# Layer 1's score matmuls: both maps' chunks in pairs, and the low queries' products on half of the array's rows each

## The chip, the cores and the metric

The kernel runs on one core of one Trainium2 chip. The metric is the device time of one execution in microseconds (us); lower is better. The kernel is written in Python against a tile framework: the program lists instructions and tiles, and the framework adds the waits, assigns buffers and orders the instructions of each engine by a plan of its own, so that the order on an engine can differ a little from the order in the program.

## The reference

Two layers over x of 2048 tokens by 1024. Layer 0 has a sliding-window attention and a chunked attention with a position bias; layer 1 has a differential attention. The change touches the scores of layer 1 alone. There, each of 8 heads has two maps of queries and keys, 64 wide:

```python
def block(i):                      # 128 queries
    qchunk = (start + jnp.arange(Q_BLOCK)) // CHUNK          # CHUNK = 64
    mask = (kchunk[None, :] <= qchunk[:, None])[None, None]
    s1 = jnp.einsum('bqhd,bkhd->bhqk', qb1, k1).astype(jnp.float32) * scale
    s2 = jnp.einsum('bqhd,bkhd->bhqk', qb2, k2).astype(jnp.float32) * scale
    p1 = jax.nn.softmax(jnp.where(mask, s1, NEG_INF), axis=-1)
    p2 = jax.nn.softmax(jnp.where(mask, s2, NEG_INF), axis=-1)
    a = p1 - lam * p2
    return jnp.einsum('bhqk,bkhd->bqhd', a.astype(v.dtype), v)
```

The result is normalised per head, multiplied by a SiLU gate, projected and added to the residual stream.

## The kernel before, in words

All of it is float32 at the borders. Products that need more than one rounded operand are split: a number is kept as a high part H and a low part L, both in a rounded 32-bit form (`F32R`), and a product is the sum of HH, HL and LH (`mm3`, lines 214 to 216: three matmuls into one PSUM bank).

Layer 0 (`project(0)`, `mix0`) and the projection of layer 1 (`project(1)`) come first. Then `_mix1` runs layer 1's attention, gates and output projection together. Names in it:

- A head `h` and a query block `b` of 512 tokens are one unit of `heads()`; the order is blocks 0 and 1 of every head, then block 2 of every head, then block 3. A block has four query tiles `j` of 128 tokens (`NTB` = 4). Query tile t = 4b + j sees (t + 1) * 128 keys, cut into chunks `z` of up to 512 keys (`cuts`); the last one can be 128, 256, 384 or 512 wide.
- `scores` makes, for each `j`, the scores of both maps `m`. The queries come in `qd` (high parts) and `ql` (low parts), each with the same 64 rows in both halves of the 128 rows. The key tile `K[z, m]` has the high part of map m's keys in rows m*64 to m*64+63 and the low part in the other 64 rows. So one matmul of `qd` with the key tile gives qH*kH + qH*kL (line 919), and one of `ql` with it gives qL*kH + qL*kL (line 920), in the same PSUM bank of the pool `pS`, which has four banks.
- After the two matmuls of a chunk, VectorE (DVE) masks 64 queries of the last chunk (line 922) and takes the row maximum `nm` (line 923); ScalarE (ACT) makes the exponential with that bias and its sum, out of PSUM into a tile `cP` (line 926), and that frees the bank. Map 0's chunks all come first, then map 1's.
- At the end of a query tile, a few small instructions make the factors `rl` and `e` (lines 934 to 940). `combine` is put off until the first exponential of the next query tile: ACT scales map 1's chunks (line 956), GpSimd (POOL) scales map 0's and adds (lines 957, 958).
- `then(j, m, z)` issues loads on SyncE's DMA queue at fixed places: the next queries at the third query tile, the next head's key tiles `ck` (lines 1044, 1045) and the values `cv` (line 1051) at the last one.
- `values` transposes the probabilities (line 970), copies them out of PSUM on DVE (line 972) and multiplies with the values (line 974). `gate` and `split` finish a head. `gates()` makes the gate's projection and `projected` the output projection, both by `mm3`; these are the side work.
- `pace` weaves the three: it takes a piece of scores (a piece says how much work it was, `yield wd / 256`), lets the values trail by `LAG1`, and hands out side work in a share of the work done (`STAGES1`). The side work's matmuls are placed behind `self.anchor`, the last score matmul issued so far (`issue_after`).

Of the kernel before, what the change touches and what calls it, by code (L numbers as in the profile page):

```python
# [10 lines left out]
F32 = mybir.dt.float32  # L11
F32R = mybir.dt.float32r
AF = mybir.ActivationFunctionType
# [5 lines left out]
P = 128  # L19
S = 2048  # L20
# [5 lines left out]
HD = 64  # L26
# [60 lines left out]
class Trunk:  # L87
# [776 lines left out]
    def _mix1(self, es):  # L864
        nc, tc, a, s = self.nc, self.tc, self.a, self.s1
        n = "c"
# [6 lines left out]
        pp = pool("pp", 20)  # L873
        kp = pool("kp", 4)
        sb = pool("sb", 2)
        NS, NTR, NO, NM = self.BANKS1
        pS = pool("pS", NS, space=PSUM)
# [3 lines left out]
        mm = nc.tensor.matmul  # L881

        def small(tag, m=1):
            return sm.tile([P, m], F32, tag=tag, name=n + tag)
# [12 lines left out]
        def scores(h, b, q, K, res, then):  # L897


            qd, ql = q  # L900
            us = res["u"] = []
            for j in range(NTB):
                t = b * NTB + j
                nk = (t + 1) * P
                cuts = [(c, min(nk, c + 512)) for c in range(0, nk, 512)]
                nb = len(cuts)
                js = slice(j * P, (j + 1) * P)
                nm = small("nm", 8).rearrange("p (m z) -> p m z", m=2)
                el = small("el", 16).rearrange("p (m z i) -> p m z i", m=2, i=2)
                e, la = el[:, :, :, 0], el[:, :, :, 1]  # L910
                l, rl = small("l", 2), small("rl", 2)
                rows = []
                for m in range(2):
                    chunks = []
                    for z, (c, ce) in enumerate(cuts):
                        wd = ce - c
                        ps = pS.tile([P, 512], F32, tag="S", name=n + "S")[:, :wd]
                        kt = K[z, m]
                        mm(ps, qd[:, m, js], kt[:, :wd], start=True, stop=False)  # L919
                        self.anchor = mm(ps, ql[:, m, js], kt[:, :wd], start=False, stop=True).ins  # L920
                        if ce == nk:
                            nc.vector.memset(ps[0:HD, wd - 64:], NEG)
                        nc.vector.tensor_reduce(nm[:, m, z:z + 1], ps, AX.X, ALU.max, negate=True)  # L923
                        chunks.append((sb if m else pp).tile([P, 512], F32, tag=f"P{m}", name=n + f"P{m}", bufs=8 if m else None))
                        acc = la[:, m, z:z + 1] if nb > 1 else l[:, m:m + 1]
                        exp = nc.scalar.activation(chunks[z][:, :wd], ps, AF.Exp, bias=nm[:, m, z:z + 1], accum_out=acc).ins  # L926
                        while parts:
                            parts.pop(0)(exp)
                        then(j, m, z)
                        yield wd / 256  # L930
                    rows.append(chunks)
                if nb > 1:
                    top, pe = small("top", 2), small("pe", 8).rearrange("p (m z) -> p m z", m=2)[:, :, :nb]
                    nc.vector.tensor_reduce(top, nm[:, :, :nb], AX.X, ALU.min)
                    for m in range(2):
                        nc.scalar.activation(e[:, m, :nb], nm[:, m, :nb], AF.Exp, bias=top[:, m:m + 1], scale=-1.0)
                    nc.vector.tensor_reduce(pe, el[:, :, :nb, :], AX.X, ALU.mult)
                    nc.vector.tensor_reduce(l, pe, AX.X, ALU.add)
                nc.vector.reciprocal(rl, l)  # L939
                nc.vector.tensor_scalar(rl[:, 1:2], rl[:, 1:2], self.nlam, None, ALU.mult)  # L940
                parts.append(lambda exp, r=(rows, cuts, e, rl): combine(exp, *r))
                us.append(rows[0])
# [3 lines left out]
        def combine(exp, rows, cuts, e, rl):  # L946

            nb = len(cuts)
            for z, (c, ce) in enumerate(cuts):
                p1, p2 = (rows[m][z][:, :ce - c] for m in range(2))  # L950
                e1, c2 = 1.0, rl[:, 1:2]
                if nb > 1:
                    e1, c2 = e[:, 0, z:z + 1], small("c2")
                    nc.vector.tensor_scalar(c2, e[:, 1, z:z + 1], rl[:, 1:2], None, ALU.mult)  # L954
                with tc.issue_after(exp) if exp is not None else nullcontext():
                    nc.scalar.activation(p2, p2, AF.Copy, scale=c2)  # L956
                nc.gpsimd.tensor_scalar(p1, p1, rl[:, 0:1], e1, ALU.mult, ALU.mult)  # L957
                nc.gpsimd.tensor_tensor(p1, p1, p2, ALU.add)  # L958
# [210 lines left out]
        def heads():  # L1169
# [7 lines left out]
            for (h, b), nxt in zip(order, order[1:] + [None]):  # L1177
                at[0] = b
                after, spare = [None, {}], NB - keys(b)
                new = nxt and nxt[0] != h  # L1180
                if nxt and not new:
                    after[1] = K

                def then(j, m, z):
                    if (j, m, z) == (2, 0, 0) and nxt:
                        after[0] = load_q(*nxt)
                    if (j, z) == (1, 0) and new:
                        for i in range(min(spare, keys(nxt[1]))):
                            after[1][i, m] = load_k(nxt[0], i, m)
                    if j == NTB - 1:  # L1190
                        if new and z + spare < keys(nxt[1]):
                            after[1][z + spare, m] = load_k(nxt[0], z + spare, m)
                        if m == 0 and z not in V:
                            V[z] = load_v(h, z)

                res = {}
                yield from scores(h, b, q, K, res, then)
                res["v"] = [V[z] for z in range(b + 1)]
                if new:
                    V = {}  # L1200
                queue.append(values(h, b, res))
                q, K = after
# [67 lines left out]
```

## Time and profile before

| | |
|---|---|
| median of 3 runs | 2809.82 us (2806.82 to 2810.93) |
| the profiled execution | 2812.16 us, span 2810.4 us |
| granted TensorE clock in it | 0.99 |
| TensorE matmuls busy | 2699.2 us (96% of the span), 13384 instructions |
| VectorE busy | 1838.0 us (65%) |
| ScalarE busy | 1629.7 us (58%) |
| GpSimd busy | 1456.0 us (52%) |
| layer 1's scores, first and last start | 1755.8 us, 2727.0 us |
| line 919, line 920 | 640 matmuls each |

PE is TensorE's matmuls and PEld its weight loads, which overlap them. A row of a group gives line, engine, operation, output and inputs, tile of the array, shapes and count, then after the bar the busy time in us, the mean duration of one in ns, and the idle time before it with what ended it. A row of the timeline begins with the start in us and the duration. A row of the waits gives the total in us, how often, and the longest. "SPq" is SyncE's DMA queue. A row of DMA issues gives the count, the size of one and the median time to landing in us.

### The profile page before, as it was taken

Reading aid. Unit: us, or ns where it says so; the run is one execution under the profiler, and the core shown is the slowest. Engines: PE = TensorE matmul, PEld = TensorE weight load, DVE = VectorE, ACT = ScalarE, POOL = GpSimd, SP = SyncE. Lnnn points to the kernel's source line nnn. Section 1 sums busy time; section 2 is a strip of 40 time slices with the busy share of each in tenths; the row PEclk is TensorE's granted clock in tenths of the full one; section 3 lists DMA queues with packets and bytes.
Section 4 is the critical chain, followed back from the end, with each engine's and each line's share of the span. In section 5 each row is a group of like instructions: output and inputs, shape, how many; then the busy total and the mean of one; then the engine's idle time right before and its main releaser. Section 6 shows DMA issues by size and latency. Waiting matters only on the chain.

```text
span 2810.4 us, 44478 instructions
## 1 busy us (share of the span) xinstructions
PE 2699.2 (96%) x13384; PEld 2168.2 (77%) x13384; DVE 1838.0 (65%) x4808; ACT 1629.7 (58%) x4135; POOL 1456.0 (52%) x1551
## 2 busy tenths in 40 slices
PE   7999999999899999899999999999999999999998
PEld 5888888888788888777788888767676777677776
DVE  8762385347777775698708870568787787777762
ACT  5443543367776775333334331678897787777761
POOL 3641251335545454267745560456676666767761
PEclk9999999999999999999999999999999999999999
DMA  5673343738877674656885435787768576455542
GB/s 183 228 238 134 112 140 116 242 109 233 238 191 189 192 195 137 213 199 219 254 254 186 143 120 161 234 248 212 221 198 240 173 214 196 131 177 153 165 151 82
DMA packets 356097, 521.72 MB, mean 186 GB/s; under 512 B 44816, under 2 KB 139792, under 8 KB 355856
## 3 DMA queue, kind: packets, MB, share of 16 engines
q1 hardware_dynamic: 355856, 518.87, 61.0%
q8 instruction: 107, 1.75, 0.3%
q14 instruction: 134, 1.10, 0.1%
HBM read 361.70 MB, written 157.02 MB: 185 GB/s over the span
## 4 chain that ended last, share of the span: by engine, by line
PE 77%; DVE 8%; DMA 7%; ACT 3%; issue 2%; POOL 1%; SPq 1%; DVEq 0%; ACTq 0%; POOLq 0%
PE cO L974 7%; PE p1mm L216 5%; PE p1mm L214 5%; PE p1mm L215 5%; PE cS L919 4%; PE p0mm L214 4%; PE cS L920 4%; PE p0mm L215 4%; PE p0mm L216 4%; PE ctr L970 3%; PE com L214 2%; PE mom L214 2%; PE com L215 2%; PE com L216 2%; PE mom L215 2%
## 5 line engine op out<-in xcount | busy, mean ns | idle before, releaser
L926 ACT ACTIVATE cP<-cS,cnm 128x512 f32<-128x512 f32 (+3 forms) x640 | 394.2, 622 | 121.9 <-DVE cnm L923 107.5
L923 DVE TENSOR_REDUCE cnm<-cS 128x1 f32<-128x512 f32 (+3 forms) x640 | 374.3, 600 | 58.2 <-PE cS L920 51.2
L958 POOL TENSOR_TENSOR cP<-cP,cP 128x512 f32<-128x512 f32 (+1 forms) x320 | 353.0, 1130 | 38.0 <-ACT cP L956 37.6
L957 POOL TENSOR_SCALAR cP<-cP,crl,cel 128x512 f32<-128x512 f32 (+3 forms) x288 | 208.8, 738 | 235.9 <-DVE crl L939 112.3
L214 PE MATMUL p1mm<-p1wH,p1hH 128*128 128x512 f32 x768 | 304.0, 396 | 5.5 <-ACT p1wH L309 5.5
L216 PE MATMUL p1mm<-p1wH,p1hL 128*128 128x512 f32 x768 | 304.7, 397 | 0.0
L215 PE MATMUL p1mm<-p1wL,p1hH 128*128 128x512 f32 x768 | 304.4, 397 | 0.1
L974 PE MATMUL cO<-cpt,cv 128*128 128x512 f32 (+3 forms) x640 | 287.7, 535 | 0.6 <-DVE cpt L972 0.5
L311 POOL TENSOR_TENSOR p0wL<-p0ws,p0wH 128x512 fp32r<-128x512 f32 (+1 forms) x124 | 149.6, 1237 | 266.7 <-ACT p0wH L309 257.5
L919 PE MATMUL cS<-ck,cqd 128*128 128x512 f32 (+3 forms) x640 | 263.9, 416 | 13.0 <-ACT cP L926 12.1
L972 DVE COPY cpt<-ctr 128x512 f32<-128x512 f32 (+1 forms) x320 | 191.2, 605 | 106.1 <-PE ctr L970 102.2
L214 PE MATMUL p0mm<-p0wH,p0hH 128*128 128x512 f32 (+1 forms) x640 | 237.8, 373 | 6.6 <-ACT p0vt L473 4.7
L216 PE MATMUL p0mm<-p0wH,p0hL 128*128 128x512 f32 (+1 forms) x640 | 237.6, 372 | 2.0 <-DVE p0hL L337 2.0
L215 PE MATMUL p0mm<-p0wL,p0hH 128*128 128x512 f32 (+1 forms) x640 | 238.0, 372 | 0.0
L920 PE MATMUL cS<-ck,cql 128*128 128x512 f32 (+3 forms) x640 | 232.1, 367 | 2.9 <-DMA cql<-qL 2.9
L311 POOL TENSOR_TENSOR p1wL<-p1ws,p1wH 128x512 fp32r<-128x512 f32 x128 | 166.5, 1321 | 123.6 <-ACT p1wH L309 113.5
L970 PEld LDWEIGHTS ctr<-ident,cP 128*128 128x128 f32 x1088 | 137.6, 141 | 115.8 <-issue 61.7
L956 ACT ACTIVATE cP<-cP,cc 128x512 f32<-128x512 f32 (+3 forms) x288 | 172.2, 662 | 16.0 <-DVE cc L954 15.5
L970 PE MATMUL ctr<-ident,cP 128*128 128x128 f32 x1088 | 175.9, 274 | 2.7 <-POOL cP L958 2.7
L214 PEld LDWEIGHTS p1mm<-p1wH,p1hH 128*128 128x128 f32 x768 | 146.0, 190 | 34.6 <-ACT p1wH L309 5.7
L215 PEld LDWEIGHTS p1mm<-p1wL,p1hH 128*128 128x128 f32 x768 | 146.0, 190 | 29.9 <-POOL p1wL L311 0.9
L216 PEld LDWEIGHTS p1mm<-p1wH,p1hL 128*128 128x128 f32 x768 | 145.8, 190 | 28.8
(301 smaller groups left out, 7070.5 us busy)
## 6 DMA issues: line engine op xcount, KB each, us to landing
p1ws<-in_od_w_in_dram SPq DMA_DIRECT2D x56, 512.0 KB, 4.2
p0ws<-in_ev_w_in_dram SPq DMA_DIRECT2D x48, 512.0 KB, 4.1
ck<-kH SPq DMA_DIRECT2D x144, 128.0 KB, 3.6
ck<-kL SPq DMA_DIRECT2D x144, 128.0 KB, 3.6
cv<-v SPq DMA_DIRECT2D x72, 256.0 KB, 4.2
cqd<-qH SPq DMA_DIRECT2D x128, 128.0 KB, 4.8
cql<-qL SPq DMA_DIRECT2D x128, 128.0 KB, 4.9
cwH<-wgH SPq DMA_DIRECT2D x64, 256.0 KB, 4.3
```

Of the source, the lines that this page charges most:

```text
L214: mm(ps, aH, bH, start=first, stop=False)
L215: mm(ps, aH, bL, start=False, stop=False)
L216: mm(ps, aL, bH, start=False, stop=last)
L311: low.tensor_tensor(l[:, :width], ws[:, k, :width], f32(h[:, :width]), ALU.subtract)
L919: mm(ps, qd[:, m, js], kt[:, :wd], start=True, stop=False)
L920: self.anchor = mm(ps, ql[:, m, js], kt[:, :wd], start=False, stop=True).ins
L923: nc.vector.tensor_reduce(nm[:, m, z:z + 1], ps, AX.X, ALU.max, negate=True)
L926: exp = nc.scalar.activation(chunks[z][:, :wd], ps, AF.Exp, bias=nm[:, m, z:z + 1], accum_out=acc).ins
L957: nc.gpsimd.tensor_scalar(p1, p1, rl[:, 0:1], e1, ALU.mult, ALU.mult)
L958: nc.gpsimd.tensor_tensor(p1, p1, p2, ALU.add)
L970: nc.tensor.transpose(tp[:, (j - j0) * P:(j - j0 + 1) * P], us[j][kt // 4][:, kk:kk + P], self.ident)
L974: mm(O[:, j0 * P:], v, T[:, :wd], start=(kt == 0), stop=(kt == nkt - 1), skip_group_check=True)
```

## The change

For every chunk `z` the two maps are made together: two banks are taken, then come both maps' matmuls with `qd` as before, on all 128 rows, and then both maps' matmuls with `ql`, each on 64 rows only: rows 0 to 63 for map 0, rows 64 to 127 for map 1, where the high part of that map's keys lies. So the product of the low queries with the low keys is left out, and only qL*kH is added. `issue_after` keeps the low matmuls in this order behind the high ones. Masks, maxima, exponentials and loads follow for map 0 and then map 1, chunk by chunk, and one `yield` hands out the work of both. The tiles and the number of all instructions stay as they were.

```diff
-                rows = []
-                for m in range(2):
-                    chunks = []
-                    for z, (c, ce) in enumerate(cuts):
-                        wd = ce - c
-                        ps = pS.tile([P, 512], F32, tag="S", name=n + "S")[:, :wd]
-                        kt = K[z, m]
-                        mm(ps, qd[:, m, js], kt[:, :wd], start=True, stop=False)
-                        self.anchor = mm(ps, ql[:, m, js], kt[:, :wd], start=False, stop=True).ins
+                rows = [[], []]
+                for z, (c, ce) in enumerate(cuts):
+                    wd = ce - c
+                    pair = [pS.tile([P, 512], F32, tag="S", name=n + "S")[:, :wd] for m in range(2)]
+                    for m, ps in enumerate(pair):
+                        self.anchor = mm(ps, qd[:, m, js], K[z, m][:, :wd], start=True, stop=False).ins
+                    for m, ps in enumerate(pair):
+                        r = slice(m * HD, (m + 1) * HD)
+                        with tc.issue_after(self.anchor):
+                            self.anchor = mm(ps, ql[r, m, js], K[z, m][r, :wd], start=False, stop=True).ins
+                    for m, ps in enumerate(pair):
                         if ce == nk:
                             nc.vector.memset(ps[0:HD, wd - 64:], NEG)
                         nc.vector.tensor_reduce(nm[:, m, z:z + 1], ps, AX.X, ALU.max, negate=True)
-                        chunks.append((sb if m else pp).tile([P, 512], F32, tag=f"P{m}", name=n + f"P{m}", bufs=8 if m else None))
+                        u = (sb if m else pp).tile([P, 512], F32, tag=f"P{m}", name=n + f"P{m}", bufs=8 if m else None)
+                        rows[m].append(u)
                         acc = la[:, m, z:z + 1] if nb > 1 else l[:, m:m + 1]
-                        exp = nc.scalar.activation(chunks[z][:, :wd], ps, AF.Exp, bias=nm[:, m, z:z + 1], accum_out=acc).ins
+                        exp = nc.scalar.activation(u[:, :wd], ps, AF.Exp, bias=nm[:, m, z:z + 1], accum_out=acc).ins
                         while parts:
                             parts.pop(0)(exp)
                         then(j, m, z)
-                        yield wd / 256
-                    rows.append(chunks)
+                    yield wd / 128
```

## The prediction

> **What bounds the kernel now.** I read the page first: the time of each engine, then the chain that ended last, then the groups of the changed lines.
>
> ```profile
> span 2810.4 us, 44478 instructions
> ...
> PE 2699.2 (96%) x13384; PEld 2168.2 (77%) x13384; DVE 1838.0 (65%) x4808; ACT 1629.7 (58%) x4135; POOL 1456.0 (52%) x1551
> ...
> PE 77%; DVE 8%; DMA 7%; ACT 3%; issue 2%; POOL 1%; SPq 1%; DVEq 0%; ACTq 0%; POOLq 0%
> ```
>
> TensorE is busy for 96% of the span and is 77% of the chain. The profiled execution took 2812.16 us, 2.34 us over the runs' median of 2809.82; I work against 2812.16 and shift by that at the end. The scores of layer 1 lie in one stretch, so I cut the span there (columns: stretch, its length, busy time of PE, PEld, DVE, ACT, POOL with counts, granted clock, DMA share, GB/s).
>
> ```profile
> 1755.00:2728.00 973.00, 942.59 (x4301) 691.89 (x4300) 722.58 (x2105) 757.28 (x2026) 639.82 (x688) 0.99 0.66 193
> 2728.00:2811.00 83.00, 73.70 (x315) 54.65 (x313) 21.38 (x40) 12.98 (x23) 18.32 (x17) 0.95 0.33 111
> ```
>
> In the 973 us with scores PE is busy for 942.59, ACT for 757.28 (78%) and DVE for 722.58 (74%). So a cut in PE's work shows in the time almost one to one, until ACT's bursts get in the way. The last 83 us have no scores and stay as they are.
>
> A matmul's printed duration is not what it costs, because the next one starts before it ends. The step from start to start is the price:
>
> ```profile
> 2302.27 0.40 PE L214 MATMUL com<-p1hH,cy 128*128 128x512 f32 x1
> 2302.51 0.39 PE L215 MATMUL com<-p1hL,cy 128*128 128x512 f32 x1
> ...
> 2304.11 0.39 PE L216 MATMUL com<-p1hH,cy 128*128 128x512 f32 x1
> 2304.33 0.39 PE L919 MATMUL cS<-ck,cqd 128*128 128x512 f32 x1
> 2304.56 0.39 PE L920 MATMUL cS<-ck,cql 128*128 128x512 f32 x1
> 2304.79 0.39 PE L214 MATMUL com<-p1hH,cy 128*128 128x512 f32 x1
> ...
> 1906.21 0.34 PE L919 MATMUL cS<-ck,cqd 128*128 128x384 f32 x1
> 1906.38 0.34 PE L920 MATMUL cS<-ck,cql 128*128 128x384 f32 x1
> 1906.56 0.39 PE L214 MATMUL cG<-p1hH,cwH 128*128 128x512 f32 x1
> ...
> 2306.11 0.19 PEld L919 LDWEIGHTS cS<-ck,cqd 128*128 128x128 f32 x1 [0.18 <-ACT cP L956]
> 2306.22 0.19 PEld L920 LDWEIGHTS cS<-ck,cql 128*128 128x128 f32 x1
> 2306.33 0.19 PEld L919 LDWEIGHTS cS<-ck,cqd 128*128 128x128 f32 x1
> ```
>
> From 2302.27 to 2304.33 are nine steps of a 512-wide matmul: 2.06 / 9 = 0.229 us. A 384-wide one steps by 0.175 (1906.21 to 1906.56 for two). Weight loads follow each other by 0.11 us, which bounds narrow chunks: a 256-wide or 128-wide chunk's two matmuls take some 0.11 us each.
>
> **The change part by part.** (1) The low queries' matmuls. Before, line 920 issues one for each chunk, and they have the forms 512 (448), 384, 256 and 128 wide (64 each):
>
> ```profile
> L920 PE MATMUL cS<-ck,cql 128*128 128x512 f32 x448 | 177.3, 396 | 2.9 <-DMA cql<-qL 2.9
> L920 PE MATMUL cS<-ck,cql 128*128 128x384 f32 x64 | 21.7, 338 | 0.0
> L920 PE MATMUL cS<-ck,cql 128*128 128x256 f32 x64 | 17.8, 281 | 0.0
> L920 PE MATMUL cS<-ck,cql 128*128 128x128 f32 x64 | 17.6, 278 | 0.0
> ```
>
> After, the same 640 are issued with 64 rows each, and map 0's takes rows 0 to 63 while map 1's takes rows 64 to 127. Each of the two writes a bank of its own. If the two run side by side, a pair costs one step in place of two, but not less than its two weight loads (2 x 0.11 = 0.22). The gain is 224 pairs x 0.229 = 51.3 us for the 512-wide, 32 x (0.35 - 0.22) = 4.2 for the 384-wide, and nothing for the 64 narrow pairs: 55 us in all. That needs the second half's weights to be loaded before its turn; the loads above run while the earlier matmul streams, so I take it as given. The other end is no gain, if the two run one after the other. I take 55, as the matmuls share neither rows nor bank; the 64-row form itself has no row in this trace.
>
> The skill draws this picture too: the Trainium skill, "TensorE: Matmul & The Clock Gate", Part 3, has matmuls on different row groups start some 4 ns apart. By that a pair would cost 0.004 us more, 1.3 us over 320 pairs, and no run so far shows it.
>
> (2) Two switches per pair, from 128-row to 64-row matmuls and back. No switch of rows is in the trace. The nearest rows are changes of another kind, from transposes in full float to the products' form:
>
> ```profile
> 2312.29 0.60 PE L970 MATMUL ctr<-ident,cP 128*128 128x128 f32 x4
> 2312.65 0.36 PE L919 MATMUL cS<-ck,cqd 128*128 128x256 f32 x1
> 2312.85 0.28 PE L920 MATMUL cS<-ck,cql 128*128 128x256 f32 x1
> 2312.96 0.40 PE L214 MATMUL com<-p1hH,cy 128*128 128x512 f32 x1
> ```
>
> Four transposes and one 256-wide matmul take 2312.29 to 2312.85 = 0.56 us, which is five steps of 0.11: that change costs nothing. Nothing is thus the lower end, as a switch has no way to gain. The upper end is that the pipeline empties before the other form starts: duration less step, 0.396 - 0.229 = 0.167 us, twice for 320 pairs = 107 us. I take a value between, nearer to the free end: the array must let the last wave pass. As an estimate, a wave through 128 rows takes as long as 128 columns take to stream, 0.229 - 0.175 = 0.054 us, and through 64 rows half of it. In and out are then 0.081 us per pair, 26 us in all.
>
> (3) The two maps' chunks together. A pair asks for two of the four banks at once, where before the second bank was asked for one chunk later (973 us / 640 = 1.52 us on average). What frees a bank is the exponential:
>
> ```profile
> L926 ACT ACTIVATE cP<-cS,cnm 128x512 f32<-128x512 f32 (+3 forms) x640 | 394.2, 622 | 121.9 <-DVE cnm L923 107.5
> L923 DVE TENSOR_REDUCE cnm<-cS 128x1 f32<-128x512 f32 (+3 forms) x640 | 374.3, 600 | 58.2 <-PE cS L920 51.2
> L956 ACT ACTIVATE cP<-cP,cc 128x512 f32<-128x512 f32 (+3 forms) x288 | 172.2, 662 | 16.0 <-DVE cc L954 15.5
> ...
> PE cS L919 <- ACT cP L926: 12.1, 16, 1.7
> PE cS L920 <- DMA cql<-qL: 2.9, 2, 2.7
> ```
>
> The exponentials, maxima and scalings are as many as before. PE waits 12.1 us for ACT in 16 places. With the second bank asked for some 1.3 us sooner, these waits grow. Lower end: nothing, or a little less than nothing, because ACT also gets its second chunk sooner. Upper end: twice as many waits, 32, each of 1.7 us, the longest seen: 54 us. ACT's 22% of free time speaks against more. I take the row once more, 12 us, because the stage's other products still stand between the pairs and ACT still has that free time. Queued behind a waiting pair on PE are the values' and the projection's products, and DVE's copies wait for those.
>
> (4) Moved DMAs. At the last of the four query tiles of a block, each pair now issues the next head's key tiles of both maps (two DMAs each) and the value tile, five in a row on SP's queue, where three came with map 0 and two with map 1 later. Their number is unchanged.
>
> ```profile
> ck<-kH SPq DMA_DIRECT2D x144, 128.0 KB, 3.6
> ck<-kL SPq DMA_DIRECT2D x144, 128.0 KB, 3.6
> cv<-v SPq DMA_DIRECT2D x72, 256.0 KB, 4.2
> 2299.51 0.52 SPq L1044 DMA_DIRECT2D ck<-kH  x1
> 2300.07 0.60 SPq L1045 DMA_DIRECT2D ck<-kL  x1
> SPq L1044 <- PE cS L920: 99.4, 55, 10.1
> ```
>
> A key tile for pair z is issued after pair z of the last row and needed four pairs later, three pairs or 9.1 us in between (six chunks of 1.52), against seven chunks before. Five issues of up to 0.60 are 3.0 us, and landing takes 3.6: 6.6 is under 9.1, so the price is nothing. The query loads stay at their place, but map 1's first pair comes at once. If the cover is gone, each of some 16 blocks late by up to 3 us costs 48; the wait would be named DMA ck.
>
> (5) The low queries still arrive in both halves of `ql`, though one half of each is read; DMA stays. The projection's products are now ordered behind a whole pair, the same in number: price nothing, as PE runs them either way. Handing out wd/128 once in place of wd/256 twice leaves the planner's shares alone.
>
> Sum: 55 - 26 - 12 = 17 us off 2812.16, so 2795; less the 2.34 above the median, 2793 us (0.6% faster).
>
> **The rivals.** (a) Switching is free. For it speak the transposes above; against it, that they keep all 128 rows. Then 55 us go, less 0 to 12 of waits: 2755 to 2767.
>
> (b) Each switch empties the pipeline: the time gets worse. The place is each of 640 switches, the price 0.167 us, so 107 - 55 = +52, with the 12 of waits +64, and 2874 us; the break-even is 55 / 640 = 0.086 us for one switch (0.067 with the waits). Half of the full price is 2820 with the waits. Against it speaks that no change of kind costs anything now; for it, that nothing else in the trace changes the array's rows. If the next weights waited as well, 0.11 more at each of 640 would be 70 us on top; I give this no place in the range.
> The Trainium skill speaks for this rival: "TensorEngine Tiling (Array Packing)", Key Properties, says that changing the tiling mode drains TensorE, while another tile in the same mode does not. It gives no figure, and no run so far shows it.
>
> (c) The two halves do not overlap, since the second one's weights come late or other work is put between them. That PE's order is not the program's shows here, where a chunk's first matmul and its second lie 0.97 us apart:
>
> ```profile
> 2306.39 0.45 PE L919 MATMUL cS<-ck,cqd 128*128 128x512 f32 x1
> 2306.68 0.59 PE L974 MATMUL cO<-cpt,cv 128*128 128x256 f32 x2
> 2307.12 0.49 PE L970 MATMUL ctr<-ident,cP 128*128 128x128 f32 x3
> 2307.36 0.48 PE L920 MATMUL cS<-ck,cql 128*128 128x512 f32 x1
> ```
>
> Then nothing is gained; with switching free and waits as today it is 2810, with the 26 and 12 of above 2848.
>
> **How the numbers follow.** A measurement of this kernel can tell about 0.2% (5.6 us) from no change. Forecast, a gain of 6 to 45 us: 0.34. (a), a gain of 45 and more: 0.22. Costs and gain cancel within 5.6 us: 0.13. (b), slower: 0.20. (c): 0.11, of which 0.02 without a change and 0.09 slower. So faster 0.56, same 0.15, slower 0.29. The range goes from (a) without waits, 2755, to 2855, which holds (c) and the half-priced (b), and leaves out the full emptying; some 0.2 lies outside. The forecast's own range is 2765 to 2804.
>
> **What would show it.** In the timeline of the changed kernel two 64-row matmuls start within 0.02 us of each other (side by side), or 0.11 apart (weights), or 0.23 (c). The step from the pair to the next 128-row matmul, over 0.229, is the price of a switch: 0 is (a), 0.05 the forecast, 0.17 (b). PE's waits for the exponentials should come to 12 to 36 us in total (24 by the forecast). ACT's and DVE's busy time should not move. What would make the forecast wrong most easily is the switch, then the waits of pairs for banks.

## The result, and the profile after

The changed kernel takes 2881.89 us (median of 4, 2874.53 to 2886.53) against 2810.38 us before (median of 4): a ratio of 1.0245, 95% interval 1.0226 to 1.0265. It is slower by 71.5 us, and the forecast was a gain of 17 us. In all that follows one execution, of the pairs on 128 rows, took 11169.8 us; its median of 2839.23 us counts it, the ratio does not, and the median of the other three is 2838.68.

The page of the changed kernel, first its span, engines and chain:

```profile
span 2878.1 us, 44398 instructions
...
PE 2764.0 (96%) x13384; PEld 2113.0 (73%) x13384; DVE 1830.2 (64%) x4808; ACT 1627.2 (57%) x4135; POOL 1455.4 (51%) x1551
...
PE 77%; DVE 8%; DMA 6%; ACT 3%; issue 2%; POOL 2%; SPq 1%; DVEq 0%; ACTq 0%; POOLq 0%
```

TensorE still carries the time, with as many instructions as before, but 65 us more of busy time (2699.2 to 2764.0). ACT and DVE do what they did. The three stretches of the span (before the scores, with them, after them) say where the 65 us lie; columns as in the prediction:

```profile
0.00:1755.00 1755.00, 1680.60 (x8782) 1419.74 (x8782) 1092.47 (x2667) 859.64 (x2087) 799.33 (x847) 0.99 0.60 185
1755.00:2795.00 1040.00, 1009.05 (x4290) 637.88 (x4289) 715.50 (x2100) 753.94 (x2023) 638.47 (x689) 0.98 0.61 180
2795.00:2879.00 84.00, 74.40 (x315) 55.36 (x314) 22.25 (x43) 13.66 (x25) 17.57 (x16) 0.95 0.33 110
```

The stretch with the scores grew from 973 to 1040 us, and PE's busy time in it from 942.6 to 1009.1, by 66.5 us; its idle time stayed (30.4 and 31.0 us). Almost the whole loss is time that the profile counts as PE's busy time, not time in which it waits. What occupies it is read from the starts in the timeline of PE's matmuls and weight loads (the first two rows are of the kernel before):

```profile
2304.34 0.19 PEld L920 LDWEIGHTS cS<-ck,cql 128*128 128x128 f32 x1
2304.56 0.39 PE L920 MATMUL cS<-ck,cql 128*128 128x512 f32 x1
...
2398.70 0.40 PE L216 MATMUL com<-p1hH,cy 128*128 128x512 f32 x1
2398.94 0.39 PE L917 MATMUL cS<-ck,cqd 128*128 128x512 f32 x1
2399.26 0.50 PE L921 MATMUL cS<-ck,cql 64*128 64x512 f32 x2
2399.69 0.50 PE L214 MATMUL com<-p1hH,cy 128*128 128x512 f32 x1
...
2306.97 0.19 PEld L921 LDWEIGHTS cS<-ck,cql 64*128 64x128 f32 x2 [0.36 <-issue]
2306.98 0.50 PE L921 MATMUL cS<-ck,cql 64*128 64x512 f32 x2
2307.41 0.19 PEld L214 LDWEIGHTS cG<-p1hH,cwH 128*128 128x128 f32 x1 [0.25 <-issue]
2307.41 0.50 PE L214 MATMUL cG<-p1hH,cwH 128*128 128x512 f32 x1
2307.52 0.19 PEld L215 LDWEIGHTS cG<-p1hL,cwH 128*128 128x128 f32 x1
2307.75 0.40 PE L215 MATMUL cG<-p1hL,cwH 128*128 128x512 f32 x1
```

Line 921 "x2" with one start and 0.50 us for both is the pair: over the trace the second of a pair starts a median of 0.003 us after the first, so the two do run side by side. But the steps around it are long. From the last 128-row matmul to the pair it is 0.32 us (2398.94 to 2399.26) in place of 0.23; from the pair to the next 128-row matmul 0.43 (2306.98 to 2307.41); and from that one to its successor 0.34 (2307.41 to 2307.75). The weight loads say why. Before, a load ran one matmul ahead (2304.34 for a matmul at 2304.56; for line 920's 512-wide ones the median lead is 0.230 us). Here the load of the pair starts with the pair (2306.97 and 2306.98), after PEld sat idle for 0.36 us, and the load of the next 128-row matmul starts with that matmul (2307.41), after 0.25 us of idle. Over all 646 switches the median lead is 0.002 us and the largest 0.031: nothing is loaded across a switch, and the load after it (2307.52) runs one loading time behind.

The medians of all such steps, 512 wide, are 0.326, 0.428 and 0.339 us, against 0.231 and 0.229 before. So a switch has two parts: 0.326 - 0.231 = 0.095 us before the other form starts, and 0.339 - 0.229 = 0.110 us because the weights behind a switch are loaded late; the pair's own step of 0.428 has both, 0.229 + 0.20. There and back cost 0.095 + 0.20 + 0.11 = 0.40 us, where a pair saves 0.229. I call the 0.095 us the emptying of the array. The trace shows only the delay: the pair starts 0.07 us before the printed end of the matmul ahead (2399.26 against 2398.94 + 0.39), and those ends are modelled.

The sum nearly closes. The trace has 323 changes to 64 rows and 323 back (six matmuls lost their partner). 323 x 0.40 = 129 us. Saved are 66 us (224 x 0.229 for the 512-wide, and 32 each x 0.175, 0.115 and 0.168 for the narrower pairs, whose two weight loads also run together). 129 - 66 = 63, and PE's busy time in the stretch grew by 66.5.

### The profile page after: what moved, and what is told of

Its sections match the earlier page's. It is cut to its first block, busy times and chain, and to the rows that moved or that the text cites. A ratio compares the mean times of both kernels' runs of the same rounds, so it can differ in the third digit from the quotient of the medians.

```text
span 2878.1 us, 44398 instructions
## 1 busy us (share of the span) xinstructions
PE 2764.0 (96%) x13384; PEld 2113.0 (73%) x13384; DVE 1830.2 (64%) x4808; ACT 1627.2 (57%) x4135; POOL 1455.4 (51%) x1551
## 4 chain that ended last, share of the span: by engine, by line
PE 77%; DVE 8%; DMA 6%; ACT 3%; issue 2%; POOL 2%; SPq 1%; DVEq 0%; ACTq 0%; POOLq 0%
PE cO L976 8%; PE p1mm L216 4%; PE p1mm L215 4%; PE p1mm L214 4%; PE cS L917 4%; PE cS L921 4%; PE ctr L972 4%; PE p0mm L214 4%; PE p0mm L216 3%; PE p0mm L215 3%; PE com L214 2%; PE cG L214 2%; PE com L216 2%; PE com L215 2%; PE mom L214 2%
## 5 line engine op out<-in xcount | busy, mean ns | idle before, releaser
L925 DVE TENSOR_REDUCE cnm<-cS 128x1 f32<-128x512 f32 (+3 forms) x640 | 363.8, 603 | 83.0 <-PE cS L921 80.8
L917 PE MATMUL cS<-ck,cqd 128*128 128x512 f32 (+3 forms) x640 | 241.7, 426 | 21.2 <-ACT cP L929 19.3
L917 PEld LDWEIGHTS cS<-ck,cqd 128*128 128x128 f32 x640 | 113.4, 192 | 57.8 <-ACT cP L929 32.0
```

What stands on the lines that cost most here:

```text
L917: self.anchor = mm(ps, qd[:, m, js], K[z, m][:, :wd], start=True, stop=False).ins
```

## The experiments

After the traces the theories stood so. **S**: the switch of rows costs 0.2 us each way, of emptying and of late weights, and the overlap works. **W**: the loss comes from pairing the chunks, by waits for banks. **N**: 64-row matmuls are slow as such, or do not overlap. **B**: 128-row and 64-row products added into one bank are what costs. Where a count of switches stands below, it is counted in that run's trace.

**The pairs on 128 rows** (two banks and the order of the change, no switch).

```diff
-                        r = slice(m * HD, (m + 1) * HD)
+                        r = slice(0, P)
```

> The changed kernel with the low queries' matmuls on all 128 rows again: both maps' chunks in pairs, no switch of rows. Theory S (each switch between 128-row and 64-row matmuls costs about 0.2 us, of which 0.1 is waiting for the array to empty and 0.1 is a weight load that nothing covers): the loss is gone, 2810 to 2822 us, with only the pairing's waits for banks left. Rival W (the loss comes from taking two banks at once and the coarser order): the loss stays, about 2880 us.

2839.23 us, ratio 1.0108 (1.0091 to 1.0124): 31 us slower than before. Neither S (0 to 12) nor W (all of it) was right on the size: the pairing alone costs, and 43 us come with the 64 rows. Its stretch with the scores, and PE's largest waits there:

```profile
1755.00:2751.00 996.00, 948.47 (x4291) 697.21 (x4291) 711.86 (x2101) 751.40 (x2024) 639.07 (x688) 0.98 0.64 188
...
PE cS L917 <- ACT cP L929: 29.7, 23, 5.8
PE cG L214 <- DMA cwH<-wgH: 6.2, 2, 4.6
PE ctr L972 <- POOL cP L960: 5.7, 7, 1.7
```

PE is idle for 47.5 of 996 us, 17 more than before; its wait for the exponentials went from 12.1 us in 16 places to 29.7 in 23, the longest from 1.7 to 5.8 us. The low matmuls stand here behind the high ones by `issue_after`, as in the change, and yet the median lead of their 512-wide loads is 0.229 us and their step 0.231. So it is the rows and not that order that makes the weights late.

**Three matmuls for a pair, without switches** (map 1's low product is left out): a stand-in for the change with free switches.

```diff
-                        self.anchor = mm(ps, qd[:, m, js], K[z, m][:, :wd], start=True, stop=False).ins
-                    for m, ps in enumerate(pair):
-                        r = slice(m * HD, (m + 1) * HD)
-                        with tc.issue_after(self.anchor):
-                            self.anchor = mm(ps, ql[r, m, js], K[z, m][r, :wd], start=False, stop=True).ins
+                        self.anchor = mm(ps, qd[:, m, js], K[z, m][:, :wd], start=True, stop=m == 1).ins
+                    with tc.issue_after(self.anchor):
+                        self.anchor = mm(pair[0], ql[:, 0, js], K[z, 0][:, :wd], start=False, stop=True).ins
```

> Pairs on 128 rows, and map 1's low product is left out: three matmuls for two chunks, as if the two low ones ran side by side and switching were free. By the steps read before (224 of 0.229, 32 of 0.175, 64 of 0.115 us) 64 us go. Theory S: 2746 to 2760 us. Rival W: 64 us off 2882, about 2818 us. If ScalarE or the banks took over as the bound once TensorE has less to do: 2775 us or more.

2788.75 us, 0.9934 (0.9917 to 0.995). Against the pairs on 128 rows 50 us go, against the kernel before only 20. It is the third of the outcomes expected, 2775 or more.

```profile
1755.00:2705.00 950.00, 898.58 (x3994) 643.27 (x3993) 711.11 (x2102) 745.95 (x2021) 641.42 (x686) 0.98 0.70 199
...
PE cS L917 <- ACT cP L927: 18.3, 30, 2.4
PE cG L214 <- DMA cwH<-wgH: 10.4, 4, 6.2
```

PE's busy time falls to 898.6, but its idle time is 51.4 us, against 30.4 in the kernel before. Even with no switch to pay for, waits take much of the gain back.

**Each chunk alone, its low matmul on 64 rows**: the kernel before with two switches for each chunk and no overlap.

```diff
-                        self.anchor = mm(ps, ql[:, m, js], kt[:, :wd], start=False, stop=True).ins
+                        r = slice(m * HD, (m + 1) * HD)
+                        self.anchor = mm(ps, ql[r, m, js], kt[r, :wd], start=False, stop=True).ins
```

> The kernel before, in its own order, with each low matmul on 64 rows (map 0 on rows 0 to 63, map 1 on rows 64 to 127), so nothing overlaps and there are two switches for each of 640 chunks, 1280 in all. Theory S: 1280 x 0.2 = 256 us more, about 3066 us (3040 to 3090). Rival W: about 2810 us, since no banks are paired. Rival N (a 64-row matmul is slow by itself, 0.1 us each): about 2880 us.

3016.86 us, 1.0747 (1.0727 to 1.0767): 208 us slower. W and N fall; S is close, 23 us under its range.

```profile
1755.00:2939.00 1184.00, 1176.16 (x4309) 693.39 (x4309) 741.01 (x2104) 778.41 (x2026) 638.89 (x689) 1.00 0.53 159
...
2300.96 0.48 PE L919 MATMUL cS<-ck,cqd 128*128 128x512 f32 x1
2301.37 0.50 PE L921 MATMUL cS<-ck,cql 64*128 64x512 f32 x1
2301.80 0.50 PE L214 MATMUL cG<-p1hH,cwH 128*128 128x512 f32 x1
2302.14 0.40 PE L215 MATMUL cG<-p1hL,cwH 128*128 128x512 f32 x1
```

The steps are those of the change, for one matmul as for a pair (0.43, then 0.34). The step into the 64 rows, 0.41, stands here behind transposes (line 971), where the same step was already longer before: medians of 0.410 and 0.314 us. PE's busy time grew by 233.6 us, 0.365 for each of 640 times there and back, a little under 0.40. Its idle time fell from 30.4 to 7.8, and its wait for the exponentials from 12.1 us to 0.9: a slower PE hardly waits for ACT. These two make the time grow by less than 256 us.

**Both low matmuls on the same 64 rows** (map 1 multiplies its low queries with its low keys).

```diff
-                        r = slice(m * HD, (m + 1) * HD)
+                        r = slice(0, HD)
```

> The changed kernel with both low matmuls on rows 0 to 63 (map 1 then multiplies its low queries with the low keys that lie there), so that the two cannot run side by side. Theory S, in which the pair overlaps fully: the second one's step comes back, 224 x 0.229 + 32 x 0.13 to 0.175 + up to 64 x 0.115 = 55 to 64 us over the changed kernel, 2937 to 2946 us. Rival N (the two never overlapped, and starts 0.003 us apart are only how the records show them): no difference, about 2882 us.

2927.81 us, 1.0434 (1.0408 to 1.0461): 46 us over the change, and 9 us under the range of S. So the overlap is real and N falls.

```profile
1755.00:2840.00 1085.00, 1067.90 (x4299) 671.50 (x4297) 718.42 (x2101) 758.40 (x2024) 637.35 (x689) 0.98 0.58 173
...
2303.01 0.73 PE L921 MATMUL cS<-ck,cql 64*128 64x512 f32 x2
2303.67 0.50 PE L214 MATMUL cG<-p1hH,cwH 128*128 128x512 f32 x1
```

The two now take 0.66 us to the next matmul, where the pair took 0.43. PE's busy time is 58.9 us over the change's, against the 55 to 64 expected, and again some idle time went (31.0 to 17.1). This run also takes the price of a switch apart, as the two steps are no longer one: by the medians of the 512-wide ones the second matmul starts 0.338 us after the first, with the late weights, and the next 128-row matmul 0.323 us after the second, with the emptying.

**What in the pairing costs**: the maps interleaved in two ways, all on 128 rows.

```diff
                 for z, (c, ce) in enumerate(cuts):
...
+                    for m in range(2):
+                        ps = pS.tile([P, 512], F32, tag="S", name=n + "S")[:, :wd]
+                        mm(ps, qd[:, m, js], K[z, m][:, :wd], start=True, stop=False)
+                        self.anchor = mm(ps, ql[:, m, js], K[z, m][:, :wd], start=False, stop=True).ins
...
-                    yield wd / 128
+                        yield wd / 256
```

> The kernel before with the maps interleaved: chunk z of map 0, then chunk z of map 1, each with its two 128-row matmuls, its own bank and its own piece (wd/256), and so the loads at the new places. Pairing cost 31 us (2839 against 2809). If taking two banks at once or the coarser pieces is what costs (P1): 2805 to 2815 us. If the order of the maps or the place of the key loads costs (P2): 2830 us or more.

2805.73 us against 2811.96, 0.9971 (0.995 to 0.9992). P2 falls: the order of the maps and the new places of the loads cost nothing. This version is even 0.3% faster than the kernel before, and the only one here that is faster without leaving a product out. With the coarser piece (`yield wd / 128` after both chunks):

> The same interleaved order, but one piece (wd/128) for both chunks, so that no side work is handed out between them; each chunk still finishes its two matmuls before the next bank is asked for in the program. If the coarser pieces cost: 2830 to 2840 us, as the pairs. If only the order of the four matmuls costs (both high, then both low): about as the interleaved one with single pieces.

2818.03 us, 1.0017 (0.9998 to 1.0036), between the two outcomes expected. Against the finer pieces the coarse one costs 12 us. The step from there to the pairs, 21 us by the medians and some 25 by the ratios (1.0017 to 1.0108), is the order of the matmuls that asks for two banks at once; the order and the banks were not taken apart. PE's waits in the two:

```profile
PE cS L917 <- ACT cP L925: 3.9, 8, 1.3
...
PE cS L917 <- ACT cP L925: 11.9, 9, 3.3
PE cG L214 <- DMA cwH<-wgH: 7.7, 2, 6.5
```

PE waits 3.9 us for the exponentials with fine pieces, 11.9 with coarse ones and 29.7 with two banks at once; in the kernel before it was 12.1.

**Fewer switches**: two chunks z together, in the order high, low, low, high.

```diff
...
+                    high(z0, pairs[0], True)
+                    low(z0, pairs[0], False)
+                    if len(zs) > 1:
+                        low(z0 + 1, pairs[1], True)
+                        high(z0 + 1, pairs[1], False)
...
```

> Two chunks z are put together: high matmuls of the first on 128 rows, low ones of the first and low ones of the second on 64 rows, then the second's high ones. A head has 24 groups in place of 40 pairs, 192 in place of 320 going in and out. Theory S (0.36 to 0.40 us for going in and out): 46 to 51 us off 2882, 2831 to 2836 us, plus waits for banks, as all four are asked for at once: up to 30 more. Rival (the cost is for each 64-row matmul and not for the switch): 2882 us or more.

2882.23 us, 1.0242 (1.0199 to 1.0285), no better than the change. By itself that is the rival's number, but the trace shows that the kernel did not do what it was meant to: other matmuls came between, as from 2307.80 to 2311.54 below, and there are 303 times there and back, not 192, with 265 pairs side by side.

```profile
2306.94 0.50 PE L917 MATMUL cS<-ck,cqd 128*128 128x512 f32 x1
2307.37 0.50 PE L924 MATMUL cS<-ck,cql 64*128 64x512 f32 x2
2307.80 1.13 PE L991 MATMUL cO<-cpt,cv 128*128 128x512 f32 x2
...
2311.54 0.50 PE L924 MATMUL cS<-ck,cql 64*128 64x512 f32 x2
2311.97 0.50 PE L917 MATMUL cS<-ck,cqd 128*128 128x512 f32 x1
```

303 x 0.40 - 265/320 x 66 = 121 - 55 = 66 us, and the span is 72 longer than before. The time alone fits S but does not decide. The groups that stayed whole do: 22 groups of four 512-wide low matmuls start at 0, 0.003, 0.338 and 0.342 us, and the next 128-row matmul at 0.664 (medians). Behind a lone pair it starts at 0.432, so the second pair adds 0.232 us, an ordinary step. A cost for each 64-row matmul would add it again, and that rival falls.

**All score matmuls on 64 rows** (the high queries times the low keys are left out, and the low product is made twice).

```diff
...
+                    for i, q1 in enumerate((qd, ql, ql)):
+                        for m, ps in enumerate(pair):
+                            r = slice(m * HD, (m + 1) * HD)
...
+                                self.anchor = mm(ps, q1[r, m, js], K[z, m][r, :wd], start=i == 0, stop=i == 2).ins
...
```

> Pairs as in the change, but every score matmul on 64 rows: map 0 on rows 0 to 63, map 1 on rows 64 to 127, three products each (the high queries, and the low queries twice), so the high queries times the low keys are left out and one product is repeated. Three side-by-side steps per pair replace two 128-row steps and one side-by-side step; the number of switches is the same. Theory S: as the change, 2874 to 2890 us. Rival B (what costs is that 128-row and 64-row matmuls add into one bank): the loss of the low products goes, 115 us off, about 2770 us.

2922.81 us, 1.0381 (1.0327 to 1.0435). B falls, as no bank mixes the two forms. S missed by 33 us; here too the plan broke the groups: 398 times there and back, and 813 of 960 pairs side by side (within 0.010 us). With these counts S gives 398 x 0.40 - 66 + 147 x 0.23 = 127 us; PE's busy time grew by 111 (1053.6 against 942.6), so the counts account for it only roughly. The groups that stayed whole show the price by itself:

```profile
1755.00:2838.00 1083.00, 1053.63 (x4941) 641.29 (x4939) 722.69 (x2101) 759.75 (x2026) 638.62 (x689) 0.98 0.59 173
...
1792.49 0.50 PE L920 MATMUL cS<-ck,cqd 64*128 64x512 f32 x2
1792.83 0.62 PE L920 MATMUL cS<-ck,cql 64*128 64x512 f32 x4
1793.38 0.50 PE L214 MATMUL cG<-p1hH,cwH 128*128 128x512 f32 x1
1793.72 0.39 PE L215 MATMUL cG<-p1hL,cwH 128*128 128x512 f32 x1
1793.95 0.39 PE L216 MATMUL cG<-p1hH,cwL 128*128 128x512 f32 x1
...
1792.49 0.19 PEld L920 LDWEIGHTS cS<-ck,cqd 64*128 64x128 f32 x2 [0.17 <-issue]
1792.59 0.42 PEld L920 LDWEIGHTS cS<-ck,cql 64*128 64x128 f32 x4
```

Six matmuls on 64 rows, two at a time. The first step is 0.34 us (1792.49 to 1792.83), as behind every switch. The other two pairs then start at 0.23 us from each other: of this group the starts are 0, 0.003, 0.338, 0.341, 0.574 and 0.577 us. So a pair inside the 64-row form costs one ordinary step of 0.23 us for two products, and only the change of form is dear. Over the 104 such groups that are 512 wide the next 128-row matmul starts at a median of 0.893 us. With the 0.095 us ahead of the group and the 0.11 behind it that is 1.10, where six matmuls on 128 rows take 6 x 0.229 = 1.37.

## Why the prediction was wrong, point by point

**What bounds it, and that PE's time shows one to one**: right for the change, where busy time grew by 66.5 us and the span by 67.7. For a gain it does not hold so well: with three matmuls in place of four PE's busy time fell by 44 us (942.6 to 898.6) and the time by 20.

**Part 1, the overlap, 55 us**: right. Of the 320 pairs 317 start 0.003 to 0.004 us apart, so rival (c) falls, and taking the overlap away added 58.9 us of busy time. The 4 ns of the Trainium skill ("TensorE: Matmul & The Clock Gate", Part 3) agree with the trace. The narrow pairs gained too, and the 128 and 256 wide ones I had put at nothing: I had priced two weight loads one after the other at 0.22 us, but the two halves' loads start a median of 0.003 us apart.

**Part 2, the switch, 26 us: this step failed.** It came to 129 us, five times as much. I priced the emptying from the time that a wave takes through the array, 0.054 and 0.027 us; it took 0.095 each way. And I took no price for the weights: I saw that before the change each load runs under the matmul ahead, and assumed that it still would across a switch. It does not, and that is another 0.11 each way. I had written down that 0.11 ("if the next weights waited as well") and given it no place in the range; with 0.095 for the emptying in place of the 0.167 bound it is what happened. The rows I called nearest, transposes to products, change no row group and told nothing on it. The break-even I gave was 0.086 us for one switch; with the 66 us that the overlap saves it is 0.10, and the switch costs 0.20. The sign I named, the step from the pair to the next 128-row matmul over 0.229, read 0.20, beyond the 0.17 of the full emptying.

The Trainium skill had the direction: "TensorEngine Tiling (Array Packing)", Key Properties, that changing the tiling mode drains TensorE. The trace agrees, with a delay of 0.095 us; that the next weights are not loaded until then, and that this is half of the price, only the runs show.

**Part 3, the pairing, 12 us**: too low by itself. The pairs on 128 rows cost 31 us: 12 for the coarser pieces and 20 to 25 for the two banks at once, less 6 to 8 that the interleaving gains. In the changed kernel it hardly shows, since a slower PE waits less for ACT, and the 12 to 36 us of waits that I named as a sign came true there:

```profile
PE cS L917 <- ACT cP L929: 19.3, 14, 5.5
```

With the pairs on 128 rows it was 29.7. The two do not add up as single prices: 31 for the pairing and then 43 for the rows, where PE's busy time says 61 (from the pairs on 128 rows) to 67 (from the kernel before) for the rows.

**Parts 4 and 5**: the moved loads cost nothing, as I said; the interleaved version has them at the same places and is not slower, and PE's waits named DMA ck come to 1.7 us in the changed kernel. Part 5's price of nothing for handing out the side work once in place of twice was wrong: that costs the 12 us above.

**The rivals**: (b) is what came, by its mechanism, at 2882 where it said 2874 for the full emptying with the waits; it reached that number with a smaller emptying and the late weights. That the two lie within 8 us is partly luck. I gave it 0.20, and cut the range at its half price. (a) would hardly have kept its 45 to 57 us: the three-matmul kernel, which stands in for it, gained 20.

## What to carry to other kernels

Count the changes between 128-row and 64-row matmuls in the order in which TensorE really runs them, at 0.40 us for there and back here; a pair of halves saves 0.23 us at 512 columns, so one pair between two switches loses, and by these prices even two pairs barely pay (0.46 against 0.40, an estimate that the whole groups of two and three pairs above bear out). Halves need long unbroken runs, and the framework's order has to keep them together. And before a load or a stall is priced at nothing because it is hidden today, ask whether the change keeps its cover: here the weights were loaded under the matmul ahead, until the form changed.

## What the runs showed of the hardware that was not expected

- After a change of the row form, the next weights load only when their matmul starts (a median lead of 0.002 us over 646 changes, against 0.230 within the 128-row form). That makes a delay of 0.095 us, which I read as emptying, and 0.11 us for the late load, each way, at a granted clock of 0.98 in that stretch. Inside one form loads run ahead, also between pairs of 64-row matmuls (steps of 0.23 us).
- Two 64-row matmuls on different rows and banks cost one step, and their weight loads run together: a 128-wide pair's step to the next matmul was 0.254 us, which is 0.20 of the switch and only some 0.05 for both products.
- Both high matmuls ahead of both low ones, which takes two of the pool's four PSUM banks at once, cost some 20 to 25 us over taking them one by one, although ACT was busy for only 75% of that stretch (751.4 of 996 us).
